# Hybrid decoder trunk, fp32, one core: the middle passes of both MLPs by seven products throughout, their two groups of blocks in alternating order

## The chip, the cores and the metric

The kernel runs on one core of one Trainium2 chip. The metric is the device time of one execution in microseconds; the profile's span, from the first to the last instruction of one profiled execution, is given beside it. Five engines matter: TensorE (PE, and PEld for its weight loads), VectorE (DVE), ScalarE (ACT), GpSimd (POOL) and SyncE (SP), which issues nearly all loads.

## The reference

Two layers over 256 positions with a model width of 2048, all in float32. Layer 0 mixes by a short gated convolution, layer 1 by latent attention; each layer ends in a squared-ReLU MLP with 8192 hidden units. Only the MLP is touched here:

```python
def sq_relu_mlp(x, w1, w2):
    return jnp.square(jax.nn.relu(x @ w1)) @ w2

def reference(...):
    ...
    for layer in range(DEPTH):
        ...
        h = layer_norm(ALPHA * h + mix, ln_g[layer, 0], ln_b[layer, 0])
        h = layer_norm(ALPHA * h + sq_relu_mlp(h, mlp_w1[layer], mlp_w2[layer]),
                       ln_g[layer, 1], ln_b[layer, 1])
    return h
```

## The kernel before, in words

**Splitting.** TensorE multiplies in a rounded form of float32. Every operand is therefore split in two: a high part (a ScalarE cast, line 127) and a low part (the operand minus the high part, a VectorE subtraction, line 128). A product of two split operands is three matmuls: high by high, high by low, low by high. In the W2 stage `dot` (line 297) emits these three, each 128x512, at lines 300, 302 and 303. Weights arrive unsplit, 128x1024 at a time (`load_raw`, line 136, five raw buffers), and are split on the chip into one of eight buffers for high parts and one of eight for low parts (`parts`, line 133).

**The stream.** `stream` lists all weight pieces in the order of use. `take` (line 183) hands out the next piece and starts the preparation of later ones, up to `LOOK = 5` steps ahead. A plain piece is one step: a load, a cast, a subtraction. A *unit* for seven products is three steps (`prepare`, line 141): two loads, a difference of 1024 columns (line 162), two of 512 (166 and 169), and splits of three pieces of 1024 and one of 512.

**The MLP.** `mlp` (line 575) goes through the hidden units in eight passes `q` of 1024. A pass has two stages.

- *W1 stage*: eight chunks of 128 hidden units, each 32 matmuls (lines 215 and 219) over 16 K tiles, into four PSUM banks in turn (`busy`). `hidden` (line 713) evacuates a chunk: a ScalarE copy (355), a VectorE addition (356), ReLU (718) and square (719) on ScalarE, and after every second chunk a split of the two chunks and `form` (line 703), which makes the four sums of activations that the seven products need.
- *W2 stage*: the hidden units times their 1024 rows of W2, giving 256 x 2048 sums that build up over the passes in SBUF (`acc`, and `sums` for the products that are not a block of the result).

The first and the last pass of a layer are plain. The six between, `FAST`, use a seven-product scheme in the manner of Strassen and Winograd: two K tiles, two halves of the positions and two column blocks of 512 make a 2x2 by 2x2 product of blocks, which takes seven block products instead of eight. The eight K tiles of a pass are four K pairs; the 2048 columns are two *groups* of two blocks. `fast_products` (line 343) does one K pair of one group: 7 products of 3 matmuls, 21 in all. The seven are named "3", "1", "5", "7", "2", "6", "4" and run in that order (`FACTORS`). Each has its own sum: "2", "3", "4" are blocks of `acc`; "1", "5", "7", "6" (`OWN`) lie in `sums`; `fold` adds these into the blocks in the last pass.

**A middle pass before.** `down_pairs` (line 634) does group 1 and then group 0, in every pass. Group 1 follows `MIXED = "sssp"`: three K pairs by seven products and the fourth plainly, that is eight products of two tiles (24 matmuls of 512 columns, one of them cut in two by `EVEN`) into the four blocks "2", "4", "22", "3". So group 1 has eight sums, which are copied from SBUF into eight PSUM banks during the W1 stage (`resume`, line 626; the copies are line 612) and put back after their last use (line 616). Group 0 does all four K pairs by seven products. Four of its sums ("3", "1", "5", "7") are copied into PSUM; the other three start from zero in PSUM, and VectorE adds them to SBUF at the end (`keep`, line 618; the addition is line 624).

**Order.** The program is written as a stream, but the order of the instructions on each engine is made by a scheduler when the kernel is built, so copies and casts of neighbouring steps are interleaved. Each engine then takes its instructions in that order. Layer 3 in the code (the second MLP) also turns the residual into the accumulator, one block pair at the start of passes 1 to 4 (`extra`, line 747).

Of the kernel before, what the change touches and what calls it, by code (L numbers as in the profile page):

```python
# [16 lines left out]
P = 128  # L17
# [17 lines left out]
NB = 4  # L35
BW = D // NB
FAST = range(1, NQ - 1)
MIXED = "sssp"
EVEN = (QC - 1, "22")
FIRST = (0, 1, 2, 3, 4, 6, 8, 12, 16)  # L40
LEAD = 4
HEAD = 4
# [11 lines left out]
def trunk(ctx: ExitStack, tc: tile.TileContext, xT, vecs, lead, w_first, w_in, w_out, w_kv, w_q, w_uk, w_uv,  # L54
# [18 lines left out]
    def halves(w):  # L73

        lead = len(w.shape) - 2
        return [(w,)] if lead == 0 else [h for i in range(w.shape[0]) for h in halves(w[i])]

    stream = []
    for m in range(NC):
        stream += halves(w_in[NC + m]) + halves(w_in[2 * NC + m]) + halves(w_in[m])  # L80
# [14 lines left out]

    stream += mlp_stream(0) + halves(w_kv) + halves(w_q)
# [44 lines left out]
    def prepare(i):  # L141

        if len(stream[i]) == 1:
            raw = load_raw(i, stream[i][0])
            hi, lo = ready[i] = parts(i)
            split(hi, lo, tiled(raw))
            yield
            return
        r1, r2 = (load_raw(f"{i}_{j}", src) for j, src in enumerate(stream[i]))
        out = []  # L150

        def finished(r, name):
            hi, lo = parts(name)
            split(hi, lo, tiled(r))
            out.append((hi, lo))

        b22, (b21, b12) = r1[:, BW:], (r2[:, :BW], r2[:, BW:])
# [4 lines left out]
        nc.vector.tensor_tensor(t.rearrange(two, a=2), b12.unsqueeze(1).to_broadcast([P, 2, BW]),  # L162
                                r1.rearrange(two, a=2), ALU.subtract)
        finished(t, f"{i}_t")
        yield
        nc.vector.tensor_tensor(b12, b22, t[:, :BW], ALU.subtract)
        finished(r2, f"{i}_2")
        t4 = r1[:, :BW]
        nc.vector.tensor_tensor(t4, b21, b12, ALU.subtract)
        f = state["fast"].tile([P, 2, BW], F32R, tag="t4", name=f"t4_{i}", bufs=2)  # L170
        split(f[:, 0, :], f[:, 1, :], t4)
        b1, t13, b2 = ([[v.rearrange("p b c -> p (b c)")[:, o:o + BW] for v in w] for o in (0, BW)] for w in out)
        ready[i] = {"11": b1[0], "22": b1[1], "21": b2[0], "T2": b2[1], "T1": t13[0], "T3": t13[1],
                    "T4": [f[:, 0, :], f[:, 1, :]]}
        yield

    def size(i):
# [174 lines left out]
    def whole(ps, out):  # L352

# [221 lines left out]
    def mlp(idx, ln, blocks, fast, begin=None, extra=None, last=False):  # L575
# [27 lines left out]
        def place(p, g):  # L603

            return sums[:, OWN.index(p), g, :] if p in OWN else \
                block(*{"2": (2 * g, 0), "3": (2 * g + 1, 0), "4": (2 * g, 1), "22": (2 * g + 1, 1)}[p])

        def resumed(p, g, name, bank):

            ps = psum(name, bank)  # L610
            if q != FAST[0] or p not in OWN:
                nc.scalar.copy(ps, place(p, g))
            return ps
# [1 line left out]
        def put_back(p, g, ps):  # L615
            nc.scalar.copy(place(p, g), ps)

        def keep(p, g, ps):

            at = place(p, g)  # L620
            if q == FAST[0] and p in OWN:
                nc.scalar.copy(at, ps)
            else:
                nc.vector.tensor_tensor(at, at, ps, ALU.add)

        def resume(busy, free, ps, m):

            b2, b3, b4, b6 = free
            b1, b5, b7, b22 = busy
            for p, bank in {3: (("3", b3),), 4: (("2", b2),), 5: (("4", b4), ("1", b1)), 6: (("6", b6), ("5", b5)),  # L630
                            7: (("7", b7), ("22", b22))}.get(m, ()):
                ps[p] = resumed(p, 1, f"ps_r{p}", bank)

        def down_pairs(h, forms, busy, free, ps):

            b2, b3, b4, b6 = free
            b1, b5, b7, b22 = busy
            new = set(OWN) if q == FAST[0] else set()
            onto = set(ps) - new
            for j, kind in enumerate(MIXED):  # L640
                if kind == "s":
                    last = j == MIXED.rindex("s")
                    fast_products(ps, h, forms, j, new if j == 0 else (), OWN if last else (), onto)
                    if last:
                        for p in OWN:
                            put_back(p, 1, ps[p])
                        then = {p: resumed(p, 0, f"ps_f{p}", bank) for p, bank in (("3", b1), ("1", b5))}
                    continue
                for two in (((0, "2"), (1, "4")), ((1, "22"), (0, "3"))):
                    w, = take(1, LOOK + 1)  # L650
                    for t, p in two:
                        for kk in range(2):
                            k = 2 * j + kk
                            dot(ps[p], wide_rows(w, kk), held(h[k], t), False, k == QC - 1, (k, p) == EVEN, True)
                    if j == len(MIXED) - 1:
                        if "5" not in then:
                            then.update({p: resumed(p, 0, f"ps_f{p}", bank) for p, bank in (("5", b7), ("7", b6))})
                        for _, p in two:
                            put_back(p, 1, ps[p])
            n = QC // 2  # L660
            onto = set(then) - new
            then.update({p: psum(f"ps_f{p}", bank) for p, bank in (("2", b2), ("6", b4), ("4", b22))})
            for j in range(n):
                fast_products(then, h, forms, j, set(then) - onto if j == 0 else (), then if j == n - 1 else (), onto)
            for p, _, _ in FACTORS:
                (put_back if p in onto or p in new else keep)(p, 0, then[p])
            return (b3, b1, b5, b7), (b6, b2, b4, b22)

        def fold():

# [12 lines left out]
            finals[n, t] = psum("ps_e", bank)  # L683
            nc.scalar.copy(finals[n, t], block(n, t))

        busy, free = (0, 1, 2, 3), (4, 5, 6, 7)
        for q in range(NQ):
            ht = act.tile([P, QC, 2 * T], F32R, tag="c", name=f"h{idx}_{q}")
            h = [ht[:, k, :] for k in range(QC)]
# [37 lines left out]
            if q == 0:  # L727
                for m in range(QC):
                    if m < GROUP:
                        if m == 0:  # L730
                            ws = ln.ws if ln.ws else group_of(GROUP)
                            if not ln.ws:
                                mm_wide(ws, ln.xd)
                            ln.finish()
                        ps = ws[m][1]
                    else:
                        ws = [(take(), psum("ps_w"))]
                        mm_wide(ws, ln.xd)
                        ps = ws[0][1]
                    hidden(m, ps, ln.weighted, AF.Relu)  # L740
                acc = act.tile([P, 2, D], F32, tag="a1", name=f"acc{idx}")
            else:
                folds = fold()
                begun = {}
                for m, ps in enumerate(products(QC, xhl, TURNED, busy)):
                    hidden(m, ps, whole)
                    if extra and m == 0 and q <= NB:
                        for t in range(2):
                            extra(block, q - 1, t, busy[2 + t])
                    if q in FAST:  # L750
                        resume(busy, free, begun, m)
                    if q == NQ - 1:
                        next(folds, None)
                        if last and m >= QC - 2:
                            for t in range(2):
                                last_sum(m - QC + 2, t, free[2 * (m - QC + 2) + t])
                        if begin:
                            begin(range(max(2 * m, 1), 2 * m + 2))

# [11 lines left out]
                    if begin and n == 1:  # L771
                        begin(range(1))
            else:
                busy, free = down_pairs(h, forms, busy, free, begun)

    def to_wide(block, put, h):

# [410 lines left out]
```

## Time and profile before

| | |
|---|---|
| time, median of 3 runs | 1999.94 us (1997.73 to 2001.57) |
| span of the profiled execution | 1994.9 us |
| TensorE, VectorE, ScalarE busy | 1987.7, 1709.4, 1354.9 us |
| granted TensorE clock | 1.000 |
| read from HBM | 381.78 MB |

A row of a timeline gives start, duration (both us), engine, line, operation, output and input, and in brackets the idle time before it with what ended it. A row of the windows gives the stretch, its length, the busy time of PE, PEld, DVE, ACT and POOL with the number of instructions, the granted clock, the share of the DMA engines and GB/s. A row of the chain gives start, duration, engine, tile and line. Durations of consecutive instructions on one engine overlap a little, so the pace of an engine is read from the distance of two starts.

### The profile page before, as it was taken

How to read it: one execution, taken by the hardware profiler on the slowest of the kernel's cores; microseconds unless marked ns; L12 is line 12 of the kernel's file. 1: busy time of each engine (PE TensorE's matmuls, PEld its weight loads, DVE VectorE, ACT ScalarE, POOL GpSimd, SP SyncE). 2: the span in 40 equal slices, each digit the busy share in tenths (PEclk: the TensorE clock that was granted, in tenths of full speed). 3: DMA queues.
4: the chain of work that ended last, by engine and by line, in shares of the span. 5: the costliest groups of instructions: out<-in, count | busy, mean ns of one | idle time of the engine just before them, and what ended most of it. 6: DMA issues, size and time to landing. Idle time of an engine off the chain costs nothing.

```text
span 1994.9 us, 30180 instructions
## 1 busy us (share of the span) xinstructions
PE 1987.7 (100%) x11110; PEld 1737.2 (87%) x11110; DVE 1709.4 (86%) x2555; ACT 1354.9 (68%) x2154; POOL 2.3 (0%) x21
## 2 busy tenths in 40 slices
PE   9999999999999999999999999999999999999998
PEld 8888888988888888888889998898888888888886
DVE  8667667797999989989978988777899999999985
ACT  6444445586778778777756755558677787887772
POOL 0000000000000000000000000000000000000000
PEclk9999999999999999999999999999999999999999
DMA  8666666565657466574855543656464656656483
GB/s 318 205 191 187 190 190 190 179 193 157 212 170 251 148 216 221 177 243 147 281 171 159 170 140 123 201 180 195 146 233 155 232 161 220 222 178 233 150 269 130
DMA packets 106853, 385.85 MB, mean 193 GB/s; under 512 B 11857, under 2 KB 12625, under 8 KB 106449
## 3 DMA queue, kind: packets, MB, share of 16 engines
q1 hardware_dynamic: 106560, 383.79, 59.5%
q8 instruction: 87, 1.43, 0.3%
q14 instruction: 62, 0.50, 0.1%
q10 hardware_dynamic: 144, 0.13, 0.0%
HBM read 381.78 MB, written 2.10 MB: 192 GB/s over the span
## 4 chain that ended last, share of the span: by engine, by line
PE 98%; DVE 1%; ACT 1%; issue 0%; DVEq 0%; ACTq 0%
PE ps_u L215 20%; PE ps_l L215 13%; PE ps_u L219 10%; PE ps_l L219 7%; PE ps_f L300 4%; PE ps_f L303 4%; PE ps_f L302 4%; PE ps_r L303 4%; PE ps_r L302 4%; PE ps_r L300 4%; PE ps_d L300 2%; PE ps_d L302 2%; PE ps_d L303 2%; PE ps_w L249 2%; PE ps_w L248 2%; PE ps_w L247 2%
## 5 line engine op out<-in xcount | busy, mean ns | idle before, releaser
L128 DVE TENSOR_TENSOR lo<-raw,hi 128x1024 fp32r<-128x1024 f32 x710 | 861.8, 1220 | 190.6 <-ACT hi L127 119.9
L127 ACT CAST hi<-raw 128x1024 fp32r<-128x1024 f32 x710 | 741.8, 1051 | 247.4 <-PE ps_l L215 98.1
L215 PE MATMUL ps_u<-xhl,hi 128*128 128x512 f32 x1792 | 621.7, 392 | 0.0
L219 PE MATMUL ps_u<-xhl,lo 128*128 128x256 f32 x1792 | 498.2, 279 | 0.0
L215 PEld LDWEIGHTS ps_u<-xhl,hi 128*128 128x128 f32 x1792 | 334.5, 187 | 73.6 <-ACT acc L595 0.2
L219 PEld LDWEIGHTS ps_u<-xhl,lo 128*128 128x128 f32 x1792 | 338.1, 189 | 1.8
L215 PE MATMUL ps_l<-xhl_a,hi 128*128 128x512 f32 x704 | 244.1, 393 | 0.0
L219 PE MATMUL ps_l<-xhl_a,lo 128*128 128x256 f32 x704 | 195.4, 279 | 0.0
L215 PEld LDWEIGHTS ps_l<-xhl_a,hi 128*128 128x128 f32 x704 | 132.1, 188 | 29.9
L219 PEld LDWEIGHTS ps_l<-xhl_a,lo 128*128 128x128 f32 x704 | 131.9, 188 | 0.2
L127 ACT CAST hi_t<-raw_t 128x1024 fp32r<-128x1024 f32 x84 | 88.5, 1054 | 45.8 <-DVE raw_t L162 41.4
L162 DVE TENSOR_TENSOR raw_t<-raw,raw 128x1024 f32<-128x1024 f32 x84 | 102.3, 1218 | 1.8 <-DMA raw<-in_w2f_dram 1.5
L128 DVE TENSOR_TENSOR lo_t<-raw_t,hi_t 128x1024 fp32r<-128x1024 f32 x84 | 102.4, 1219 | 0.2
L718 ACT ACTIVATE fp<-fp 128x256 f32<-128x256 f32 x96 | 40.0, 416 | 63.2 <-DVE fp L356 62.6
L215 PE MATMUL ps_l<-z,hi 128*128 128x512 f32 x240 | 82.4, 391 | 0.0
L300 PE MATMUL ps_d<-hi,h 128*128 128x512 f32 x192 | 75.0, 391 | 0.0
L302 PE MATMUL ps_d<-lo,h 128*128 128x512 f32 x192 | 75.0, 390 | 0.0
L303 PE MATMUL ps_d<-hi,h 128*128 128x512 f32 x192 | 74.8, 389 | 0.0
L249 PE MATMUL ps_w<-xd,hi 128*128 128x258 f32 x256 | 72.7, 284 | 0.0
L248 PE MATMUL ps_w<-xd,lo 128*128 128x258 f32 x256 | 72.3, 282 | 0.0
L247 PE MATMUL ps_w<-xd,hi 128*128 128x258 f32 x256 | 72.3, 282 | 0.0
L215 PE MATMUL ps_l<-oT,hi 128*128 128x512 f32 x208 | 71.3, 391 | 0.0
(296 smaller groups left out, 3963.7 us busy)
## 6 DMA issues: line engine op xcount, KB each, us to landing
raw<-in_w_dram SPq DMA_DIRECT2D x344, 512.0 KB, 4.5
raw<-in_w2f_dram SPq DMA_DIRECT2D x168, 512.0 KB, 3.9
raw<-in_w_in_dram SPq DMA_DIRECT2D x88, 512.0 KB, 4.2
raw<-in_w_out_dram SPq DMA_DIRECT2D x32, 512.0 KB, 3.7
raw<-in_w_o_dram SPq DMA_DIRECT2D x32, 512.0 KB, 4.2
raw<-in_w_kv_dram SPq DMA_DIRECT2D x10, 512.0 KB, 3.7
raw<-in_w_q_dram SPq DMA_DIRECT2D x8, 512.0 KB, 4.0
raw<-in_w_uk_dram SPq DMA_DIRECT2D x8, 512.0 KB, 3.9
```

Source lines behind the costliest of these rows:

```text
L127: nc.scalar.copy(hi, src)
L128: nc.vector.tensor_tensor(lo, src, hi.bitcast(F32), ALU.subtract)
L162: nc.vector.tensor_tensor(t.rearrange(two, a=2), b12.unsqueeze(1).to_broadcast([P, 2, BW]), r1.rearrange(two, a=2), ALU.subtract)
L215: nc.tensor.matmul(ps, w[blk // 8][0][:, blk % 8, :], x, start=first, stop=False)
L219: nc.tensor.matmul(ps[:, :T], w[blk // 8][1][:, blk % 8, :], x[:, :T], start=False, stop=last)
L247: nc.tensor.matmul(ps[:, :W], hi, x[k][:, :W], start=k == 0, stop=False)
L248: nc.tensor.matmul(ps[:, :W], lo, x[k][:, :W], start=False, stop=False)
L249: nc.tensor.matmul(ps[:, :W], hi, x[k][:, W:], start=False, stop=k == NC - 1)
L300: nc.tensor.matmul(ps, x[0], w[0], start=first, stop=False, skip_group_check=onto)
L302: nc.tensor.matmul(ps[:, at], x[0], w[1][:, at], start=False, stop=False, skip_group_check=onto)
L303: nc.tensor.matmul(ps, x[1], w[0], start=False, stop=last, skip_group_check=onto)
L718: nc.scalar.activation(f, f, AF.Relu)
```

## The change

All twelve middle passes (six in each MLP) change in the same way.

- All four K pairs of both groups go by seven products: `MIXED`, `EVEN` and the plain pair go away, and so does the sum "22" during the middle passes.
- The order of the groups alternates: `groups(q)` is (1, 0) in the first middle pass, (0, 1) in the second, and so on. The second group of one pass is the first of the next.
- The sums "3", "1", "5", "7" of the second group stay in their PSUM banks over the next W1 stage. "2", "6", "4" are put back and copied in again at W1 chunks 4, 5, 6, into banks that W1 has done with.
- In the first group's last K pair, each sum is put back as its product ends (`turn`), and the bank that it leaves takes the second group's sum of the next product. All seven sums of the second group start from copies; no addition by VectorE (`keep`) is left.
- In the second MLP the residual is turned into the blocks in the order 0, 2, 1, 3.
- In `prepare` the code that makes the unit's fourth piece moves into a helper; the operations stay.

```diff
-MIXED = "sssp"
-EVEN = (QC - 1, "22")
...
+    def groups(q):
+        return (1, 0) if (q - FAST[0]) % 2 == 0 else (0, 1)
...
-            for j, kind in enumerate(MIXED):
-                out += [(w2f[l, q, 1, j, 0], w2f[l, q, 1, j, 1])] if kind == "s" else \
-                    halves(w2[l, q, 2, j]) + halves(w2[l, q, 3, j])
-            out += [(w2f[l, q, 0, j, 0], w2f[l, q, 0, j, 1]) for j in range(QC // 2)]
+            for i, g in enumerate(groups(q)):
+                for j in range(QC // 2):
+                    out.append((w2f[l, q, g, j, 0], w2f[l, q, g, j, 1]))
...
-    def fast_products(ps, x, forms, j, fresh, ready, onto=()):
+    def fast_products(ps, x, forms, j, fresh, ready, onto=(), then=None):
...
             dot(ps[p], b[r], a[l], p in fresh, p in ready, onto=p in onto)
+            if then:
+                then(p)
...
+        def first_sums(ps, banks, m):
+            g = groups(q)[0]
+            for p in {0: ("3", "1", "5", "7") if q == FAST[0] else (), 4: "2", 5: "6", 6: "4"}.get(m, ()):
+                banks.setdefault(p, busy[m % 4])
+                ps[p] = resumed(p, g, f"ps_r{p}", banks[p])
...
+        def down_pairs(h, forms, ps, banks, spare):
+            first, second = groups(q)
+            new = set(OWN) if q == FAST[0] else set()
             n = QC // 2
+            order = [p for p, _, _ in FACTORS]
+            after, place_of = {}, {}
+            def begin_next(p, bank):
+                after[p], place_of[p] = resumed(p, second, f"ps_f{p}", bank), bank
+            def turn(p):
+                put_back(p, first, ps[p])
+                i = order.index(p) + 1
+                if i < len(order):
+                    begin_next(order[i], banks[p])
+            def end(p):
+                if q == FAST[-1] or p not in order[:4]:
+                    put_back(p, second, after[p])
             for j in range(n):
+                if j == n - 1:
+                    begin_next(order[0], spare)
+                fast_products(ps, h, forms, j, new if j == 0 else (), ps if j == n - 1 else (), set(ps) - new,
+                              turn if j == n - 1 else None)
+            stay = order[:4] if q < FAST[-1] else []
+            for j in range(n):
+                fast_products(after, h, forms, j, new if j == 0 else (), after if j == n - 1 else (),
+                              set(order) - new, end if j == n - 1 else None)
...
-                            extra(block, q - 1, t, busy[2 + t])
+                            extra(block, (0, 2, 1, 3)[q - 1], t, busy[2 + t])
                     if q in FAST:
-                        resume(busy, free, begun, m)
+                        first_sums(sums_in, places, m)
```

More of the change, by code (lines that the diff above doesn't have):

```diff
@@ L148, in prepare @@
             return
-        r1, r2 = (load_raw(f"{i}_{j}", src) for j, src in enumerate(stream[i]))
         out = []
@@ L155, in finished, with fourth, named @@
             out.append((hi, lo))
+        def fourth(src):
+            f = state["fast"].tile([P, 2, BW], F32R, tag="t4", name=f"t4_{i}", bufs=2)
+            split(f[:, 0, :], f[:, 1, :], src)
+            return [f[:, 0, :], f[:, 1, :]]
+        def named(names):
+            return {n: [v.rearrange("p b c -> p (b c)")[:, o:o + BW] for v in w]
+                    for w, pair in zip(out, names) for n, o in zip(pair, (0, BW))}
+        r1, r2 = (load_raw(f"{i}_{j}", src) for j, src in enumerate(stream[i]))
         b22, (b21, b12) = r1[:, BW:], (r2[:, :BW], r2[:, BW:])
@@ L169, in prepare @@
         nc.vector.tensor_tensor(t4, b21, b12, ALU.subtract)
[L170 to L174, printed above, removed]
+        ready[i] = {**named((("11", "22"), ("T1", "T3"), ("21", "T2"))), "T4": fourth(t4)}
         yield
@@ L616, in put_back @@
             nc.scalar.copy(place(p, g), ps)
[L618 to L632, printed above, removed]
@@ L634, in down_pairs @@
-        def down_pairs(h, forms, busy, free, ps):
-            b2, b3, b4, b6 = free
-            b1, b5, b7, b22 = busy
-            new = set(OWN) if q == FAST[0] else set()
[L639 to L659, printed above, removed]
-            n = QC // 2
-            onto = set(then) - new
-            then.update({p: psum(f"ps_f{p}", bank) for p, bank in (("2", b2), ("6", b4), ("4", b22))})
-            for j in range(n):
[L664 to L667, printed above, removed]
@@ new lines, in down_pairs @@
+        def down_pairs(h, forms, ps, banks, spare):
+            first, second = groups(q)
+            new = set(OWN) if q == FAST[0] else set()
+            n = QC // 2
+            order = [p for p, _, _ in FACTORS]
[10 more added lines that the diff above has]
+                    put_back(p, second, after[p])
+            for j in range(n):
+                if j == n - 1:
[6 more added lines that the diff above has]
+                              set(order) - new, end if j == n - 1 else None)
+            if stay:
+                return [banks[order[-1]]] + [place_of[p] for p in order[4:]], {p: after[p] for p in stay}, \
+                    {p: place_of[p] for p in stay}
+            return [banks[order[-1]]] + [place_of[p] for p in order[:3]], {}, {p: place_of[p] for p in order[3:]}
@@ L684, in last_sum @@
             nc.scalar.copy(finals[n, t], block(n, t))
-        busy, free = (0, 1, 2, 3), (4, 5, 6, 7)
+        busy, sums_in, places = (0, 1, 2, 3), {}, {"3": 4, "1": 5, "5": 6, "7": 7}
         for q in range(NQ):
@@ L755, in mlp @@
                             for t in range(2):
-                                last_sum(m - QC + 2, t, free[2 * (m - QC + 2) + t])
+                                last_sum(m - QC + 2, t, list(places.values())[2 * (m - QC + 2) + t])
                         if begin:
@@ L773, in mlp @@
             else:
-                busy, free = down_pairs(h, forms, busy, free, begun)
+                busy, sums_in, places = down_pairs(h, forms, sums_in, places, busy[3])
     def to_wide(block, put, h):
```

1 line of the change is left out of this document (removed).

## The prediction

> **What bounds the kernel now.** First the page: the span, the busy times, and the chain that ended last.
>
> ```profile
> span 1994.9 us, 30180 instructions
> ...
> PE 98%; DVE 1%; ACT 1%; issue 0%; DVEq 0%; ACTq 0%
> ```
>
> The chain is TensorE nearly throughout, so at first sight any matmul taken away is time won. A matmul's busy time overlaps that of the next, so TensorE's pace is read from starts. The timeline of one middle pass of layer 1 (it begins at 536.00, the next at 619.23) shows them:
>
> ```profile
> 536.00 0.39 PE L215 MATMUL ps_u<-xhl,hi 128*128 128x512 f32 x1
> ...
> 594.72 0.39 PE L300 MATMUL ps_r<-hi,h 128*128 128x512 f32 x1
> ...
> 600.19 0.39 PE L300 MATMUL ps_f<-hi,forms 128*128 128x512 f32 x1
> ...
> 604.95 0.39 PE L300 MATMUL ps_f<-hi,forms 128*128 128x512 f32 x1
> ...
> 616.06 0.39 PE L302 MATMUL ps_f<-lo_t,forms 128*128 128x512 f32 x1
> ...
> 619.23 0.39 PE L215 MATMUL ps_u<-xhl,hi 128*128 128x512 f32 x1
> ```
>
> The pass takes 83.23 us. The plain K pair (594.72 to 600.19, 25 matmuls) takes 5.47; a pair by seven products (600.19 to 604.95, 21 matmuls) 4.76, or 0.227 a matmul.
>
> Next the busy times by window: two whole passes, then the first of them cut at the fourth W1 chunk's end, at the end of VectorE's idle spells, and at the W2 stage's start (580.4).
>
> ```profile
> 536.00:619.20 83.20, 83.20 (x429) 71.28 (x428) 78.09 (x101) 66.44 (x104) 0.00 (x0) 1.00 0.60 199
> 619.20:702.40 83.20, 83.20 (x429) 71.25 (x428) 80.13 (x104) 67.42 (x103) 0.00 (x0) 1.00 0.64 207
> 536.00:558.20 22.20, 22.20 (x129) 19.55 (x128) 18.20 (x23) 18.51 (x29) 0.00 (x0) 1.00 0.91 328
> 558.20:563.40 5.20, 5.20 (x32) 4.58 (x31) 4.45 (x6) 2.73 (x6) 0.00 (x0) 1.00 0.46 120
> 563.40:580.40 17.00, 17.00 (x101) 14.99 (x100) 16.82 (x28) 13.91 (x26) 0.00 (x0) 1.00 0.30 89
> 580.40:619.20 38.80, 38.80 (x174) 32.15 (x173) 38.63 (x46) 31.30 (x46) 0.00 (x0) 1.00 0.58 184
> ```
>
> After the window's length come PE, PEld, DVE and ACT busy. **VectorE is busy 78.1 and 80.1 of the 83.2 us**, mean 79.1; and from 563.4 to the end, 55.45 of 55.8. TensorE bounds the pass, but VectorE has no room from the middle of W1 to the end of W2. Its timeline there:
>
> ```profile
> 563.48 1.23 DVE L128 TENSOR_TENSOR lo<-raw,hi 128x1024 fp32r<-128x1024 f32 x1 [0.83 <-ACT hi L127]
> ...
> 611.32 1.22 DVE L162 TENSOR_TENSOR raw_t<-raw,raw 128x1024 f32<-128x1024 f32 x1
> 612.57 0.69 DVE L166 TENSOR_TENSOR raw<-raw,raw_t 128x512 f32<-128x512 f32 x1
> 613.30 0.69 DVE L169 TENSOR_TENSOR raw<-raw 128x512 f32<-128x512 f32 x1
> 613.91 1.22 DVE L128 TENSOR_TENSOR lo_t<-raw_t,hi_t 128x1024 fp32r<-128x1024 f32 x1
> 615.04 1.22 DVE L128 TENSOR_TENSOR lo<-raw,hi 128x1024 fp32r<-128x1024 f32 x1
> 616.18 0.68 DVE L128 TENSOR_TENSOR t<-raw,t 128x512 fp32r<-128x512 f32 x1
> 616.78 1.22 DVE L128 TENSOR_TENSOR lo<-raw,hi 128x1024 fp32r<-128x1024 f32 x1
> ```
>
> This is the last unit of the pass. Its lo_t is done at 613.91 + 1.22 = 615.13; TensorE reads it at 616.06. **The margin is 0.93 us.** At the end of layer 1 it is already gone; the chain there leaves TensorE and comes back to it over a ScalarE copy that a matmul waited for:
>
> ```profile
> 937.43 0.49 ACT acc L616
> 937.97 0.50 PE ps_f L300
> ```
>
> **The change part by part.** There are twelve middle passes, six a layer.
>
> *TensorE.* Each pass trades the plain pair for one more unit: 5.47 - 4.76 = 0.71 us less, 12 x 0.71 = 8.5 us in all. Nothing is added to it; the copies that start a sum in PSUM run on ScalarE.
>
> *VectorE.* One more unit costs two differences and its splits. From the rows: 611.32 to 616.78 is 5.46, and the unit's first split 1.13 (613.91 to 615.04), together 6.6. The plain pair's two splits go, 2 x 1.13 = 2.3. The three additions of L624 go as well, since those sums now start from a copy; their pace is
>
> ```profile
> 619.05 0.68 DVE L624 TENSOR_TENSOR acc<-acc,ps_f 128x512 f32<-128x512 f32 x1
> 619.65 0.68 DVE L624 TENSOR_TENSOR sums<-sums,ps_f 128x512 f32<-128x512 f32 x1
> ```
>
> or 0.60 each, 1.8 in all. Net **+2.5 us of VectorE a pass**: 79.1 + 2.5 = 81.6, where TensorE would need 83.2 - 0.7 = 82.5. That leaves 0.9 us for idleness, and VectorE now idles 3.1 or 5.1 a pass (83.2 minus the window rows, mean 4.1). Nearly all of it falls before 563.4 (22.20 - 18.20 = 4.0 up to 558.2). By the bracket of the row at 563.48 such a spell is a wait for a ScalarE cast, and a cast needs, by the code, one of eight weight buffers that TensorE has finished with: running ahead is capped, so work can't be drawn forward at will. The additions removed lie behind the last unit, so they don't help it.
>
> The same by the window that decides: from 563.48 to the last lo_t, work grows by 6.6 - 2.3 = 4.3 and the matmul comes 0.7 earlier: 5.0 against a margin of 0.93. The 0.83 idle may go, because the instruction order now puts the fourth chunk's addition and a difference ahead of the first unit's split. That leaves the lo_t 3.2 us late. Some is covered: the built order puts other products' high matmuls ahead of the waiting low one. But the unit's later parts and the next pass's first split, queued behind it, are as late, and TensorE needs them next. So the pass stretches until VectorE fits: 81.6 + idle. With the lesser idle (3.1) it is 84.7, +1.5; with the mean (4.1) 85.7, **+2.5**. I take the mean, for nothing favours one of the two. 12 x 2.5 = 30; bounds so far 12 x 1.5 = 18 and, if the idle went, -8.5.
>
> *ScalarE.* Four sums stay in PSUM, but "22" no longer is one; a pass has 10 copies in and 10 out where it had 12 and 12. A unit's casts come on top. Total load is no matter (66 of 83.2), its order is. Before, copies lie scattered between casts:
>
> ```profile
> 591.52 0.59 ACT L616 COPY sums<-ps_r 128x512 f32<-128x512 f32 x1 [1.52 <-PE ps_r L303]
> 592.13 0.59 ACT L612 COPY ps_f<-acc 128x512 f32<-128x512 f32 x1
> 593.15 1.06 ACT L127 CAST hi_t<-raw_t 128x1024 fp32r<-128x1024 f32 x1 [0.42 <-DVE raw_t L162]
> ...
> 595.58 1.55 ACT L616 COPY sums<-ps_r 128x512 f32<-128x512 f32 x3
> 597.01 0.61 ACT L612 COPY ps_f<-sums 128x512 f32<-128x512 f32 x1
> ```
>
> Now 13 copies belong to the last unit of the first group: each sum is put back when its product ends, and its bank reloaded for the next product. In the built order seven stand in a row ahead of the cast for T1 and T3 of the second group's second unit, and five more ahead of that unit's last large cast. A copy goes every 0.48 (595.58 to 597.01 is three): 12 x 0.48 = 5.8 us of casting held up within two units, 9.5 of TensorE. How much of it reaches VectorE no row shows. Bounds: nothing, if the casts stay ahead of VectorE; at most 5.8; and an estimate from following the order at these paces, 1.7 us of VectorE idleness a pass, at the two casts behind the copies. I take nothing for the forecast, since VectorE has its own backlog to work off meanwhile, and 1.7 for a rival.
>
> In the row at 591.52 the copy waits 1.52 us for TensorE, and no cast starts until it is through. The Trainium skill, "TensorE: Matmul & The Clock Gate", Part 1 (on the engines' queues), makes a rule of it: ScalarE and VectorE take their queues strictly in order. By that rule a put-back that waits for a product holds every cast behind it, and the 1.7 would be due in full; if casts could overtake, nothing would.
>
> *The rest.* The loads move the same bytes. W1's order, the fold and the last pass's sums keep their counts. The order of the residuals in layer 3 changes, not their number.
>
> Sum: 1994.9 + 30 = **2024.9 of span**. The runs' median, 1999.94, lies 5.0 above the profiled span, so 2030.
>
> **The rivals.**
>
> *TensorE stays the bound.* The gain of 8.5 us arrives: 1999.9 - 8.5 = 1991. For it: the chain, and the lead that VectorE could gather in early W1. Against it: 55.45 of 55.8 us busy, and 4.3 us more in that stretch. It decides if the pass has under 0.9 us of VectorE idle left.
>
> *A draw.* VectorE's lateness just eats the 0.71: margin and idle together absorb all but that. Time within 0.2% (4 us, what a measurement can tell from no change) of 1999.9.
>
> *The copies hold up the casts.* Forecast's stretch plus 1.7 a pass: 12 x 4.2 = 50, 2050. For it: the wait of 1.52 in the row at 591.52, with the casts behind it. Against it: before, no cast held up so stopped TensorE in these passes, and ScalarE has 17 us to spare in each. It decides once the T1/T3 cast starts after its difference is done.
>
> *It doesn't do what it says.* The sums held over W1 save only four ScalarE copies a pass, 1.9 us on an engine that doesn't bound it; that part then has no effect on time. It is inside all cases.
>
> **How the numbers follow.** Forecast (+1.5 to +3.3 a pass, the upper end with half the copies' 1.7) 0.64: 2030, own range 2018 to 2040. Copies 0.20: 2050. TensorE the bound 0.11: 1991. Draw 0.05. Slower 0.84, same 0.05, faster 0.11. The range leaves the last two out and reaches over the copies' 2050 for what isn't counted: 2006 to 2054.
>
> **What would show it.** In the changed profile: middle passes of 85 to 87 us between W1 starts; VectorE at 81 a pass and full from mid-W1; TensorE idle in the second group, waiting for the low parts or the casts of the units; the two lines of the split in the chain that ended last, with shares of more than 1%. If copies matter, VectorE idles over 1 us in the second group, waiting for hi. A pass of 82.5 with TensorE never idle would prove me wrong, as would VectorE busy below 80 a pass.

## The result, and the profile after

The changed kernel takes 2049.59 us (median of 4 runs, 2047.74 to 2050.06) against 1999.25 (1997.73 to 2001.57) for the kernel before on the same chip: a ratio of 1.0251, 95% interval 1.0236 to 1.0265, that is 50 us more. The prediction was 2030 in a range of 2006 to 2054; the rival "the copies hold up the casts" named 2050.

The page after, the lines that answer to those shown of before:

```profile
span 2046.0 us, 30047 instructions
...
PE 78%; DVE 9%; ACT 8%; issue 3%; DMA 2%; DVEq 0%; ACTq 0%; SPq 0%
PE ps_u L221 16%; PE ps_l L221 13%; PE ps_u L225 8%; PE ps_l L225 7%; DVE lo L129 4%; ACT hi L128 3%; PE ps_f L308 2%; PE ps_d L306 2%; PE ps_d L309 2%; PE ps_d L308 2%; PE ps_f L309 2%; PE ps_f L306 2%; ACT ps_f L627 2%; PE ps_w L255 2%; DVE raw_t L172 2%
```

TensorE has fallen from 98% of the chain to 78%; VectorE (9%) and ScalarE (8%) have taken most of the rest. The lines named are VectorE's splits (L129, 4%), ScalarE's casts (L128, 3%), the copies into PSUM (L627, 2%) and the 1024-column differences (L172, 2%). The windows of two successive middle passes of the first MLP (layer 1 in the code), from the same point of one W1 stage to the next (columns as before: length, PE, PEld, DVE, ACT busy):

```profile
539.12:626.78 87.66, 85.84 (x426) 69.79 (x425) 81.86 (x105) 66.38 (x101) 0.00 (x0) 1.00 0.57 192
626.78:714.44 87.66, 85.81 (x426) 69.76 (x425) 81.79 (x105) 66.23 (x101) 0.00 (x0) 1.00 0.58 193
```

A pass takes 87.66 us where it took 83.23. VectorE is busy 81.8 of them (79.1 before), close to the 81.6 worked out; it is idle 5.8. TensorE now is idle for 1.8 by this row, though its busy time also covers matmuls that start late behind the one before: it has work for 82.5 only, so it loses 5.1. Which waits those are is in the list of waits of the first of these passes (us in total, how often, the longest):

```profile
DVE lo L129 <- ACT hi L128: 5.0, 6, 1.3
ACT acc L631 <- PE ps_f L309: 3.1, 2, 2.8
...
PEld ps_f L306 <- ACT hi_t L128: 1.7, 2, 1.3
PEld ps_f L308 <- DVE lo L129: 1.6, 3, 0.6
PEld ps_f L306 <- ACT hi L128: 1.4, 3, 0.7
```

TensorE's weight loads wait for high parts of units, which ScalarE makes (3.1 us in these rows), and for low parts, which VectorE makes (1.6); VectorE itself waits 5.0 for ScalarE's casts, and a put-back waits up to 2.8 for TensorE. The place where the two engines meet is the turn between the groups. ScalarE's timeline there:

```profile
604.28 1.11 ACT L627 COPY ps_f<-sums 128x512 f32<-128x512 f32 x2
605.32 0.59 ACT L631 COPY sums<-ps_f 128x512 f32<-128x512 f32 x1
605.80 0.59 ACT L631 COPY acc<-ps_r 128x512 f32<-128x512 f32 x1
606.27 1.06 ACT L128 CAST hi_t<-raw_t 128x1024 fp32r<-128x1024 f32 x1
607.22 0.60 ACT L627 COPY ps_f<-acc 128x512 f32<-128x512 f32 x1
607.74 0.60 ACT L627 COPY ps_f<-sums 128x512 f32<-128x512 f32 x1
608.26 0.60 ACT L631 COPY sums<-ps_r 128x512 f32<-128x512 f32 x1
608.74 0.61 ACT L631 COPY acc<-ps_r 128x512 f32<-128x512 f32 x1
609.22 0.62 ACT L627 COPY ps_f<-acc 128x512 f32<-128x512 f32 x1
609.74 1.08 ACT L128 CAST hi<-raw 128x1024 fp32r<-128x1024 f32 x1
```

and VectorE's idle time in the same stretch:

```profile
610.85 1.23 DVE L129 TENSOR_TENSOR lo<-raw,hi 128x1024 fp32r<-128x1024 f32 x1 [0.99 <-ACT hi L128]
...
616.71 1.23 DVE L129 TENSOR_TENSOR lo<-raw,hi 128x1024 fp32r<-128x1024 f32 x1 [0.44 <-ACT hi L128]
```

From 604.3 to 609.7 ScalarE does one cast and nine copies. The cast of 609.74 comes behind the last of them, and VectorE, in the middle of the stretch where it has no time to spare, stands 0.99 us for it, then 0.44 once more: 1.4 of its 5.8 idle. (The cast that ended the 0.44 comes behind no copy: it had itself waited 2.4 us for a matmul.)

Not every middle pass grew alike. The first of the first MLP, then its last, after and before:

```profile
453.03:537.01 83.98, 82.62 (x419) 68.96 (x418) 73.25 (x97) 57.87 (x90) 0.00 (x0) 1.00 0.48 146
888.12:979.91 91.79, 88.95 (x432) 72.10 (x430) 84.59 (x108) 69.45 (x107) 0.00 (x0) 0.98 0.59 193
```

```profile
868.91:953.06 84.15, 83.69 (x429) 71.12 (x428) 78.52 (x102) 66.34 (x103) 0.00 (x0) 1.00 0.59 198
```

From W1 start to W1 start, the first pass of each MLP grew by 0.8 us, the four inner ones by 4.4 to 4.9 in the first MLP and by 3.7 to 5.1 in the second, the last by 7.6 and 6.5: 50 us together. Where VectorE has 73.3 us to do (the first), the change costs next to nothing; where it has 84.6 (the last), it costs most.

### The profile page after: what moved, and what is told of

Read it like the earlier page. It is cut to its first block, busy times and chain, and to the rows that moved or that the text cites. A ratio compares the mean times of both kernels' runs of the same rounds, so it can differ in the third digit from the quotient of the medians.

```text
span 2046.0 us, 30047 instructions
## 1 busy us (share of the span) xinstructions
PE 2015.8 (99%) x11062; PEld 1721.8 (84%) x11062; DVE 1741.0 (85%) x2581; ACT 1356.0 (66%) x2142; POOL 2.3 (0%) x21
## 4 chain that ended last, share of the span: by engine, by line
PE 78%; DVE 9%; ACT 8%; issue 3%; DMA 2%; DVEq 0%; ACTq 0%; SPq 0%
PE ps_u L221 16%; PE ps_l L221 13%; PE ps_u L225 8%; PE ps_l L225 7%; DVE lo L129 4%; ACT hi L128 3%; PE ps_f L308 2%; PE ps_d L306 2%; PE ps_d L309 2%; PE ps_d L308 2%; PE ps_f L309 2%; PE ps_f L306 2%; ACT ps_f L627 2%; PE ps_w L255 2%; DVE raw_t L172 2%
## 5 line engine op out<-in xcount | busy, mean ns | idle before, releaser
L129 DVE TENSOR_TENSOR lo<-raw,hi 128x1024 fp32r<-128x1024 f32 x710 | 860.9, 1219 | 204.5 <-ACT hi L128 133.2
L128 ACT CAST hi<-raw 128x1024 fp32r<-128x1024 f32 x710 | 740.2, 1050 | 276.3 <-PE ps_l L221 98.4
L221 PE MATMUL ps_u<-xhl,hi 128*128 128x512 f32 x1792 | 628.9, 396 | 0.0
L221 PEld LDWEIGHTS ps_u<-xhl,hi 128*128 128x128 f32 x1792 | 335.4, 188 | 79.1 <-ACT acc L603 0.2
L128 ACT CAST hi_t<-raw_t 128x1024 fp32r<-128x1024 f32 x96 | 101.3, 1056 | 83.6 <-DVE raw_t L172 65.1
L172 DVE TENSOR_TENSOR raw_t<-raw,raw 128x1024 f32<-128x1024 f32 x96 | 116.9, 1218 | 4.3 <-DMA raw<-in_w2f_dram 4.0
L129 DVE TENSOR_TENSOR lo_t<-raw_t,hi_t 128x1024 fp32r<-128x1024 f32 x96 | 117.0, 1218 | 1.0 <-ACT hi_t L128 0.8
L306 PE MATMUL ps_f<-hi_t,forms 128*128 128x512 f32 x176 | 67.6, 406 | 12.4 <-ACT hi_t L128 12.4
```

The lines of the kernel that those rows point to most:

```text
L128: nc.scalar.copy(hi, src)
L129: nc.vector.tensor_tensor(lo, src, hi.bitcast(F32), ALU.subtract)
L221: nc.tensor.matmul(ps, w[blk // 8][0][:, blk % 8, :], x, start=first, stop=False)
L306: nc.tensor.matmul(ps, x[0], w[0], start=first, stop=False, skip_group_check=onto)
```

## The experiments

In all of them "before" is the kernel before, run on the same chip at the same time; the times stand beside 1998 to 2000 for it.

**No copies at the turn.** In the four inner middle passes of each layer:

```diff
+            bare = q not in (FAST[0], FAST[-1])
...
-                after[p], place_of[p] = resumed(p, second, f"ps_f{p}", bank), bank
+                after[p], place_of[p] = psum(f"ps_f{p}", bank) if bare else resumed(p, second, f"ps_f{p}", bank), bank
...
-                put_back(p, first, ps[p])
+                if not bare:
+                    put_back(p, first, ps[p])
...
-                fast_products(after, h, forms, j, new if j == 0 else (), after if j == n - 1 else (),
-                              set(order) - new, end if j == n - 1 else None)
+                fast_products(after, h, forms, j, (set(order) if bare else new) if j == 0 else (),
+                              after if j == n - 1 else (), () if bare else set(order) - new, end if j == n - 1 else None)
```

> The changed kernel without the 13 ScalarE copies at the turn between the groups, in eight of its twelve middle passes (the four inner ones of each layer): there the first group's sums are not put back and the second group's start from zero, so those sums are left out of the output. VectorE's and TensorE's work stays. If VectorE's load alone stretches the pass (the forecast's own step, copies worth nothing), the time stays at 2050 within 4 us. If the copies hold up the casts (the rival), each of the eight passes loses the 1.7 to 1.9 us and the time is 2034 to 2036. If TensorE's waits were for something else, no change either.

Measured: 2035.83 us, ratio 1.0179 (1.0163 to 1.0194), 13.8 below the changed kernel. The windows of two of the passes concerned:

```profile
541.16:627.21 86.05, 84.69 (x426) 70.21 (x424) 81.67 (x105) 59.75 (x87) 0.00 (x0) 1.00 0.58 196
627.21:713.25 86.04, 84.66 (x426) 70.17 (x425) 81.55 (x105) 59.40 (x87) 0.00 (x0) 1.00 0.59 196
```

87.66 has become 86.05: **1.6 us a pass**, with VectorE as busy as before the cut, and its idle time down from 5.8 to 4.4. Its waits for casts in this pass are

```profile
DVE lo L129 <- ACT hi L128: 3.7, 4, 1.3
```

so the two waits at the turn are gone. The copies cost what the rival said: 1.6 us by these passes, 13.8 / 8 = 1.7 by the medians. (The run profiled is the slowest of the four, 2041.07, 5 us above the other three, so its span is not used for this.) What is left, 86.05 against 82.5, is not due to the copies at the turn.

**Less work for VectorE.** One 512-column difference of each unit left out, then both:

```diff
-        nc.vector.tensor_tensor(b12, b22, t[:, :BW], ALU.subtract)
...
-        nc.vector.tensor_tensor(t4, b21, b12, ALU.subtract)
```

The run with one less drops the second of the two lines (`t4`), the other run both.

> The changed kernel without the second of the two 512-column differences in each unit, that is 8 x 0.60 = 4.8 us of VectorE work less in a middle pass; the fourth product's weights are then wrong. Copies stay. If VectorE's load sets the pass (87.65 us now), the pass falls by the whole 4.8 to about 82.9, and the time by 57 to about 1993. If the copies are a limit of their own beside VectorE, the pass stops at 82.5 + 1.7 = 84.2 and the time at about 2008. If VectorE is no bound, the time stays at 2050.

> The changed kernel without both 512-column differences in each unit: 9.6 us of VectorE work less in a middle pass; four of the seven products' weights are then wrong. If VectorE's load sets the pass, TensorE is the bound again, the pass is 82.5 and the time 1999.9 - 8.5 = 1991 (no further fall than that). If the copies are a limit of their own, 2008 as with one difference less.

Measured: 2004.15 (1.0020, 1.0010 to 1.0029) with one less, 1998.33 (0.9988, 0.9978 to 0.9997) with two. A middle pass with one less:

```profile
620.67:704.31 83.64, 83.56 (x426) 70.23 (x424) 76.77 (x97) 67.18 (x101) 0.00 (x0) 1.00 0.62 201
```

4.8 us less for VectorE bring the pass down by 4.0 and the time by 45: VectorE's load is the larger limit. They don't bring it to 82.5, nor does the run with two; something beside VectorE's load is left, but less than the 1.7 a pass that a limit of its own would leave.

**Both cuts together.**

```diff
-        nc.vector.tensor_tensor(b12, b22, t[:, :BW], ALU.subtract)
...
-        nc.vector.tensor_tensor(t4, b21, b12, ALU.subtract)
...
+            bare = q not in (FAST[0], FAST[-1])
...
```

The lines on `bare` that are not shown are those of the run without copies.

> Both cuts together: no turn copies in eight passes, and neither 512-column difference in any unit; both parts are left out of the output. With VectorE and the copies gone as limits the eight passes are at TensorE's 82.5. Time 1991 if VectorE's load is the only limit (the same as without the copies' cut); if the copies limit by themselves, 1991 + 4 x 1.7 = 1998 against 2008 with the copies in.

Measured: 1992.89 us, ratio 0.9957 (0.9942 to 0.9972). A pass without copies:

```profile
619.89:702.40 82.51, 82.51 (x425) 70.67 (x424) 71.48 (x88) 59.38 (x86) 0.00 (x0) 1.00 0.61 203
```

That is TensorE's own time, 82.5, to the digit worked out: the matmuls removed are worth 0.71 us a pass once nothing else is in the way. The copies cost 5.4 us over eight passes here, 0.7 each, where they cost 1.6 with VectorE full. They are dear because they fall on a VectorE without slack.

**Seven products alone.** The kernel before with one part of the change:

```diff
-MIXED = "sssp"
+MIXED = "ssss"
...
-                    fast_products(ps, h, forms, j, new if j == 0 else (), OWN if last else (), onto)
+                    fast_products(ps, h, forms, j, new if j == 0 else (), ps if last else (), onto)
                     if last:
-                        for p in OWN:
-                            put_back(p, 1, ps[p])
-                        then = {p: resumed(p, 0, f"ps_f{p}", bank) for p, bank in (("3", b1), ("1", b5))}
+                        then = {}
+                        for p, q2, bank in (("3", None, None), ("1", "3", b1), ("5", "1", b5), ("7", "5", b7),
+                                            ("2", None, None), ("6", "7", b6), ("4", None, None)):
+                            put_back(p, 1, ps[p])
+                            if q2:
+                                then[q2] = resumed(q2, 0, f"ps_f{q2}", bank)
```

> The kernel before with one part of the change alone: all four K pairs of group 1 by seven products, the groups in fixed order, no sum kept over W1, the three VectorE additions at the end of group 0 still there. It computes everything. VectorE's work grows by 4.3 us a pass against before (1.8 more than in the changed kernel), TensorE's falls by 0.71, and 11 copies meet at the turn. If VectorE's load sets the pass: 79.1 + 4.3 + 4.1 of idle = 87.5, plus the copies' 1.7 = 89.2, 12 x 6.0 = 72, time 2072, slower than the changed kernel. If the window alone decides (the additions lie behind the last unit), the same as the changed kernel, 2050. If kept sums and alternation are what costs the time, 1991.

Measured: 2045.33 us, ratio 1.0235 (1.0219 to 1.0251), 4 below the changed kernel. So seven products for the fourth pair, with the copies at the turn that come with them, cost nearly all of the time, and the sums kept over W1 with the alternating groups give none of it back. (The two intervals overlap, so the 4 us between them is not settled.) The windows of two passes:

```profile
625.48:712.67 87.19, 84.77 (x425) 70.33 (x424) 83.47 (x108) 67.15 (x103) 0.00 (x0) 1.00 0.58 194
712.67:799.84 87.17, 84.76 (x426) 70.27 (x425) 83.56 (x108) 67.30 (x103) 0.00 (x0) 1.00 0.58 193
```

VectorE does 1.7 us more here than in the changed kernel, for the three additions, and the pass is no longer for it: its idle time is 3.7 in place of 5.8. Additions behind the last unit cost nothing that this comparison can show (the two kernels differ in their copies as well), as the view by the full window has it; the view by "busy plus a constant idle", which gave 2072, is wrong.

**More work for VectorE in the kernel before.** The first 512-column difference of each unit done twice, and then in two units of a pass only:

```diff
         nc.vector.tensor_tensor(b12, b22, t[:, :BW], ALU.subtract)
+        nc.vector.tensor_tensor(b12, b22, t[:, :BW], ALU.subtract)
```

```diff
+        unit = state["units"] = state.get("units", -1) + 1
...
         nc.vector.tensor_tensor(b12, b22, t[:, :BW], ALU.subtract)
+        if unit % 7 in (4, 5):
+            nc.vector.tensor_tensor(b12, b22, t[:, :BW], ALU.subtract)
```

> The kernel before with one thing added: each unit's first 512-column difference is computed twice (same inputs, same output), 7 x 0.60 = 4.2 us more of VectorE work a middle pass; TensorE, copies and sums as before, and the output as well. If VectorE's load stretches the pass, 79.1 + 4.2 + 4.1 = 87.4, that is 12 x 4.2 = 50, time 2050; by the window with its margin of 0.93, 12 x 3.3 = 39, time 2039. If VectorE has room that the forecast didn't see, 2000.

> The kernel before with the repeated 512-column difference in two units of each pass (the second and third of the second group): 1.2 us more of VectorE work a middle pass; all is computed. With the forecast's margin of 0.93 us a pass absorbs most of it: 12 x 0.27 = 3, time 2002. In proportion to the run with 4.2 us more (34 us), without any margin, 10 us, time 2009. If the margin is larger than read, 1999.

Measured: 2032.26 (1.0169, 1.0154 to 1.0184) with 4.2 us more, 2007.89 (1.0046, 1.0034 to 1.0058) with 1.2 us more. Two passes of the first:

```profile
626.31:712.98 86.67, 85.47 (x429) 70.99 (x428) 83.38 (x110) 66.95 (x103) 0.00 (x0) 1.00 0.59 195
712.98:799.27 86.29, 85.06 (x429) 71.05 (x428) 83.31 (x110) 67.40 (x104) 0.00 (x0) 1.00 0.58 194
```

With no part of the change in it, work on VectorE alone brings these passes of the kernel before from 83.2 to 86.3 and more, and the time up by 34 us: 2.8 a pass, of the 4.2 given. Two units with 0.6 more each cost 9.3 us, 0.78 a pass of 1.2. The passes absorbed 1.4 us in one run and 0.4 in the other, so no fixed room, neither 0.93 nor another, fits both; in both about two thirds of what was added came out (0.68 and 0.65), close to the "in proportion" of the second expectation. In the second run TensorE waited not for lo_t, from which the margin was read, but for the low part of the unit's third piece, by the list of waits over the whole execution:

```profile
PEld ps_f L305 <- DVE lo L128: 10.9, 14, 1.1
```

In the kernel before that operand had more room than lo_t: it is done at 615.04 + 1.22 = 616.26 and read at 617.42. One pass later lo_t itself is done at 696.01 + 1.22 = 697.23 and read at 699.28, 2.05 us later:

```profile
617.42 0.39 PE L302 MATMUL ps_f<-lo,h 128*128 128x512 f32 x1
...
696.01 1.22 DVE L128 TENSOR_TENSOR lo_t<-raw_t,hi_t 128x1024 fp32r<-128x1024 f32 x1
...
699.28 0.39 PE L302 MATMUL ps_f<-lo_t,forms 128*128 128x512 f32 x1
```

In the run with 1.2 us more, VectorE takes the differences between the two splits, and the third piece waits for its cast as well:

```profile
618.46 1.23 DVE L128 TENSOR_TENSOR lo<-raw,hi 128x1024 fp32r<-128x1024 f32 x1 [0.53 <-ACT hi L127]
...
619.74 0.50 PE L305 MATMUL ps_f<-lo,h 128*128 128x512 f32 x1 [0.77 <-DVE lo L128]
```

The 0.93 was the slack of one operand in one pass, in an order that another program does not keep.

**A step less of look-ahead in the kernel before.**

```diff
-LOOK = 5
+LOOK = 4
```

> The kernel before with the look-ahead of the stream cut from 5 steps to 4 (plain pair: from 6 to 5); all work stays. A step is about 2.1 us of VectorE work. If the lead gathered before the full window is what carries a pass (window view, margin 0.93 us), a step less turns the margin into -1.2 us: 12 x 1.2 = 14, time 2014. If VectorE's load over the whole pass decides (79.1 of 83.2), the lead matters little and the time stays within 4 us of 2000.

Measured: 2005.17 us, ratio 1.0029 (1.0018 to 1.0040). Half of the window view's cost, and more than none: a lead counts, but a step less of it is not 2.1 us later at the last unit. A pass of it, and TensorE's waits over the whole execution:

```profile
627.00:710.45 83.45, 83.45 (x429) 71.14 (x428) 78.96 (x103) 66.33 (x103) 0.00 (x0) 1.00 0.59 203
```

```profile
PEld ps_f L302 <- DVE lo_t L128: 8.0, 13, 1.3
```

The wait is for lo_t, the operand named, but the pass went from 83.23 to 83.45 only, 0.2 where 1.2 was expected. Seven of the twelve middle passes grew by this 0.2; most of the 6.6 us comes from two, one in each MLP, that grew by 2.3 and 2.5.

**Two tries to relieve VectorE with GpSimd**, both on the changed kernel: the two 512-column differences of each unit, and the four 128-column additions of the activation sums.

```diff
-        nc.vector.tensor_tensor(b12, b22, t[:, :BW], ALU.subtract)
+        nc.gpsimd.tensor_tensor(b12, b22, t[:, :BW], ALU.subtract)
...
-        nc.vector.tensor_tensor(t4, b21, b12, ALU.subtract)
+        nc.gpsimd.tensor_tensor(t4, b21, b12, ALU.subtract)
```

```diff
-                nc.vector.tensor_tensor(s1, a21, a22, ALU.add)
-                nc.vector.tensor_tensor(s3, a21, a11, ALU.subtract)
-                nc.vector.tensor_tensor(s2, s1, a11, ALU.subtract)
-                nc.vector.tensor_tensor(s4, a12, s2, ALU.subtract)
+                nc.gpsimd.tensor_tensor(s1, a21, a22, ALU.add)
+                nc.gpsimd.tensor_tensor(s3, a21, a11, ALU.subtract)
+                nc.gpsimd.tensor_tensor(s2, s1, a11, ALU.subtract)
+                nc.gpsimd.tensor_tensor(s4, a12, s2, ALU.subtract)
```

> The changed kernel with both 512-column differences of each unit on GpSimd in place of VectorE; it computes everything. If GpSimd does them beside VectorE without disturbing it and in less than about 2 us each, the time is that of the kernel with both left out, 1998, a little under before. If the two engines slow each other down, or GpSimd is late with the unit's third step, it lies between 1998 and 2050 or above. This is a try at a version that beats both, not a test of the theories; VectorE's theory expects at least half of the 52 us back if VectorE's own instructions keep their durations.

> The changed kernel with the four 128-column additions of the activation sums (16 a pass, 16 x 0.205 = 3.3 us of VectorE) on GpSimd; it computes everything. If VectorE's load sets the pass and GpSimd disturbs nothing: 12 x 3.3 = 39 less, 2010; if only those of them that lie in the full window count (11 of 16, 2.3 us), 2022. If the copies are all that matters, 2050.

Measured: 2132.14 (1.0670, 1.0652 to 1.0688) and 2101.68 (1.0517, 1.0501 to 1.0533), both slower than the changed kernel. The groups by shape, of the run with the differences on GpSimd (count, busy us, mean ns, idle before):

```profile
L179 POOL TENSOR_TENSOR raw<-raw 128x512 f32<-128x512 f32 x96 | 172.4, 1796 | 80.4 <-DVE lo L129 43.0 <-DMA raw<-in_w2f_dram 13.1 <-issue 11.3
...
L129 DVE TENSOR_TENSOR lo_t<-raw_t,hi_t 128x1024 fp32r<-128x1024 f32 x96 | 143.2, 1491 | 51.0 <-ACT hi_t L128 50.6
```

The second difference takes GpSimd 1.80 us in the mean (the first, L176, 1.61), against 0.69 on VectorE in the changed kernel, and this subtraction of VectorE's 1.49 in place of 1.22. The 2 us of the condition are kept in the mean; that VectorE is not disturbed is not. GpSimd is late, too: ScalarE's casts of the fourth piece waited for it 36 times, 53.6 us in all. TensorE's own largest wait is for neither, but for copies at the turn that reload a PSUM bank, and its granted clock falls after it (the waits of the whole execution, one such wait, and two windows of 2 us around it):

```profile
PE ps_f L306 <- ACT ps_f L627: 38.4, 13, 4.3
```

```profile
619.53 0.80 PE L306 MATMUL ps_f<-hi,h 128*128 128x512 f32 x1 [4.28 <-ACT ps_f L627]
```

```profile
612.00:614.00 2.00, 2.00 (x11) 1.65 (x10) 0.88 (x2) 1.05 (x1) 1.08 (x1) 1.00 0.91 322
622.00:624.00 2.00, 2.00 (x7) 1.52 (x6) 2.00 (x1) 2.00 (x5) 1.19 (x1) 0.50 0.00 0
```

Before the wait of 4.28 us a window holds 11 matmuls at a granted clock of 1.00, after it 7 at 0.50. The mean clock of this run is 0.986, of the run with the additions 0.981, of the changed kernel 0.999. By these means some 28 of the 83 us lost against the changed kernel, and some 38 of the 52, would be clock; this is an estimate (the difference of the clocks times the span). So the two losses are not the price of GpSimd's slower arithmetic alone, and how they divide is open.

No run beat the kernel before with all of the work in it; the two that did, 1993 and, by 0.1%, 1998, leave parts out.

## Why the prediction was right, and where its size was off

The prediction's point, 2030, is 20 us low. The measured 2049.6 lies outside the forecast's own 2018 to 2040 and at the time of the rival "the copies hold up the casts", which had a chance of 0.20; the stated range holds it because it was drawn out to 2054 over that rival. The direction and the engine were right, one term of the sum was not. The signs named in advance came (VectorE busy 81.8, its splits and the casts in the chain with over 1%, VectorE idle for 1.4 us at the turn); only the pass, 87.66, is longer than the 85 to 87.

- **What bounds the kernel.** Right. TensorE was nearly the whole chain, and yet VectorE had hardly any room: 1.2 us more of VectorE work a pass is felt in the kernel before.
- **TensorE's term** (-0.71 us a pass): right, 82.51 once the other limits are gone.
- **VectorE's load** (+2.5 us of work, "81.6 + idle", 85.7 a pass): the load is 81.8 measured; without copies the pass is 86.05, so the stretch is 2.8 where 2.5 was forecast. The number held, its derivation only half, and so in part by luck. The step "So the pass stretches until VectorE fits: 81.6 + idle ... I take the mean" treats the idle as a constant; over the runs in which VectorE limits the pass it is 3.0 to 3.7 with 83.3 to 83.6 us of work, and 4.4 and 5.8 with 81.6 to 81.9, without and with the copies at the turn. The mean taken, 4.1, happened to be near the 4.4. The other derivation, by the window from 563.48 to the last unit, is borne out in what it counts: 4.3 us more and no credit for the additions, and the run with seven products alone, with the additions still in it, was not slower. Its fixed margin of 0.93 is not: it gave 3.3, 0.27 and 1.2 us a pass for the three runs that tested it on the kernel before, and 2.8, 0.78 and 0.55 were measured (by the times). (The prediction says that a unit costs "two differences and its splits"; the rows it adds up hold three differences, and the sum is right. The copy at 937.43 that a matmul waited for puts back a sum, so it says nothing on the margin of a low part.)
- **The copies.** Here the size failed: "I take nothing for the forecast, since VectorE has its own backlog to work off meanwhile". The runs show 1.6 us a pass in place of nothing. A backlog does not help when the next piece of it needs the cast that is held up: VectorE takes its instructions in order and stood 0.99 us at 610.85. The casts did not overtake the copies: the source of the cast at 609.74 was ready at about 606.7 (VectorE's first 512-column difference ran from 606.02, 0.69 us), and five copies went first. The estimate kept for the rival, 1.7, was the size to take, though not quite for its reason: of the two casts it named, that of T1 and T3 started 0.3 us after its difference and did not stop VectorE; the other cost the 0.99. Together 2.8 + 1.6 = 4.4 a pass, which is the growth of an inner pass. That 12 x 4.4 = 53 comes near the 51 by which the span grew is a balance of first passes (+0.8) and last ones (+7.6 and +6.5). The last ones also put back the four sums that stay in the others; no run separates what they lose.
- **The kept sums** were said to save only ScalarE copies, without effect. Borne out as far as the runs go: the version without them, and without the alternation, is no slower, and 4 us faster by its median, which the intervals don't settle.
- **The rivals.** "TensorE stays the bound" and "a draw" fall. "The copies hold up the casts" is what happened, on top of the forecast's own stretch and not in its place.

Open: how much of the remaining 0.7 us a pass of the copies, with VectorE relieved, is a reload that TensorE itself waits for, and how much is a late cast. In the run without both differences the largest wait of the weight loads is for the reloads, ahead of that for the casts of T1 and T3 (hi_t, 3.8 us):

```profile
PEld ps_f L304 <- ACT ps_f L625: 6.8, 12, 1.3
```

That speaks for the reload, but a weight load's wait is not all lost to the matmuls, which waited 2.0 us for these copies. Every edit also changes the order that the scheduler makes on each engine, so a few tenths of a microsecond a pass between two experiments can't be put down to one edit.

## What to carry to other kernels

A chain that is 98% one engine does not mean that time taken from that engine is won: before trading work from it to another, count how long the other is busy in the stretch where the trade takes place, from the point where its lead is capped to the last operand that it must deliver. If it is full there, most of what is added comes out at the end: here about two thirds of a microsecond for each one added, and 4.0 of the 4.8 taken away came back. On engines that work in order, copies that wait for a product should not be bunched ahead of the casts that the next products need; their price is largest when the engine behind those casts has no slack.

## What the runs showed of the hardware

GpSimd is no free helper beside a busy VectorE. An addition of 128 x 128 in float32 took it 0.80 to 0.98 us in the mean of a line, where VectorE needed 0.28 in the changed kernel, and a split of VectorE's grew, as the groups of the run with the additions on GpSimd show:

```profile
L709 POOL TENSOR_TENSOR sf<-fp,sf 128x128 f32<-128x128 f32 x48 | 47.0, 979 | 3.8
...
L706 POOL TENSOR_TENSOR sf<-fp 128x128 f32<-128x128 f32 x48 | 38.1, 795 | 235.0 <-ACT fp L718 235.0
```

```profile
L129 DVE TENSOR_TENSOR h<-fp,h 128x512 fp32r<-128x512 f32 x48 | 45.3, 943 | 0.0
```

The last row is VectorE's split of the activations, 0.68 us in the kernel before. The means hide two cases. In one place of the same run an addition takes 0.47 us while VectorE waits for most of it, and the next 1.35 while VectorE splits:

```profile
652.64 0.47 POOL L708 TENSOR_TENSOR sf<-sf,fp 128x128 f32<-128x128 f32 x1
653.18 1.35 POOL L709 TENSOR_TENSOR sf<-fp,sf 128x128 f32<-128x128 f32 x1
```

```profile
654.13 0.95 DVE L129 TENSOR_TENSOR h<-fp,h 128x512 fp32r<-128x512 f32 x1
```

The Trainium skill, "GPSIMD Engine Reference", section "Specifications", says that the two engines share their SBUF interfaces, and that they contend with VectorE instructions that have two SBUF inputs. The run with the differences on GpSimd agrees:

```profile
597.49 2.17 POOL L179 TENSOR_TENSOR raw<-raw 128x512 f32<-128x512 f32 x1
```

```profile
596.30 2.19 DVE L129 TENSOR_TENSOR lo_t<-raw_t,hi_t 128x1024 fp32r<-128x1024 f32 x1
598.42 0.41 DVE L364 TENSOR_TENSOR fp<-ps_u,t 128x256 f32<-128x256 f32 x1
```

A split of 128 x 1024, with two SBUF inputs, takes 2.19 us beside GpSimd's differences in place of 1.22; the addition behind it, which reads one operand from PSUM, takes 0.41 while GpSimd is still at work, as in the changed kernel (0.42). GpSimd's own difference takes 2.17 there, and 1.28 at 620.54, where VectorE is idle.
